# The second product of the MLP: for six of eight output tiles, twelve of 22 chunks by 2x2 blocks with seven products each

## The chip, the cores and the metric

One core of a Trainium2 chip. The metric is the device time of one execution in microseconds (us); the kernel before took 664.03 us, the median of three runs (663.77 to 664.38).

## The reference, cut to what matters

One transformer block on 512 tokens, D = 1024, in float32: attention, then a gated MLP with a causal convolution, then a gated per-layer input. The change is in the product with `w_down`, whose inner size is D_FF = 2816 = 22 chunks of 128:

```python
gu = h @ w_gate_up[i]
a, u = jnp.split(gu, [D_FF], axis=-1)
a = causal_dwconv(a, conv_w[i], conv_b[i])
y = (jax.nn.gelu(a, approximate=True) * u) @ w_down[i]     # (512 x 2816) @ (2816 x 1024)
x = x + rmsnorm(y, mlp_post_g[i])
e = p[i] @ w_ple[i]
x = x + e * jax.nn.sigmoid(x @ w_ple_gate[i])
```

## The kernel before

Everything is held transposed: features on the 128 partitions, the 512 tokens along the free axis. Every fp32 product is made of three fp32r matmuls, since each operand is split into a high and a low half: `mm3` (L138 to L149) issues hi·hi (L145), lo·hi (L148) and hi·lo (L149), each with a 128x128 weight and 512 (or 256) columns of tokens.

`weight()` brings a weight in: SP issues the load into one of two `wr` buffers (L138), ACT copies the high half out (L126), DVE subtracts it to get the low half (L130). The halves live in six `wh` slots, so three weights of up to 1024 columns; the split of a weight waits until PE is done with the weight three before it, and the next load waits until a split has freed its `wr`.

`mlp_up` makes the 22 chunks of the MLP's inner vector. `mlp_tile(j)` (L1006 to L1022) leaves chunk j as a pair of halves in `self.y[j]`; the first four chunks come from one joint product, the rest one by one. `mlp_down` multiplies them with `w_down`: for each of eight output tiles `c`, three weights of 1024, 1024 and 768 columns (8, 8 and 6 chunks) are loaded, split and multiplied into one PSUM bank with 22 x 3 matmuls of 512 columns. DVE copies the bank out (L1092), ACT squares it (L266) and POOL adds the square to a running sum (L267) for the RMS norm. The last tile, c = 7, is done in two halves of 256 tokens, so that the norm of the first half runs under the second half's matmuls (`last`, `out`). Three of the gate's weights (`wpg`, loaded at c = 2, 3 and 4, and split into free slots of other buffers) and a fourth wait for the product of the gate that follows; `norm_half` adds the normed result to x (`self.x1`, four tiles of 128x2x512), and `gated` adds e (`self.e`, p @ w_ple, four such tiles).

The instruction order on each engine comes from the framework's scheduler, which orders by priority and its own timing; instructions given to `keep_in_program_order` (`keep`, `load_late`) stay in the order of the code. Within a queue nothing overtakes.

## Time and profile before

| | |
|---|---|
| median of 3 runs | 664.03 us (663.77 to 664.38) |
| the profiled execution | 663.63 us, of which the span is 661.8 us |
| granted TensorE clock | 0.999 of full speed |
| PE, share of the span | 99% |
| DVE / ACT / POOL | 61% / 49% / 25% |
| second product of the MLP | 490.0 to 611.9 us of the span |
| DMA | 69.56 MB, mean 105 GB/s |

Matmuls are pipelined, so the duration in a matmul's row (0.39 us at 512 columns) is not what it adds: that is the distance from one start to the next. All times in rows are us from the start of the span, unless marked ns.

### The profile page before, as it was taken

The page shows a single profiled execution, that of the slowest core. Times are in us where ns is not written, and L with a number is a line of the kernel's source. Part 1 is how long each engine was busy: PE and PEld are TensorE (multiplying, and loading weights), DVE is VectorE, ACT ScalarE, POOL GpSimd, SP SyncE. Part 2 cuts the span into 40 slices and gives each one's busy share as a digit, 9 for nine tenths or more (in the row PEclk, how much of TensorE's full clock was granted, in tenths as well). Part 3 has the DMA queues.
Part 4 walks back from the last instruction along what each step waited for, and adds up shares of the span by engine and source line. Part 5 has one row for each costly group of instructions (what it writes and reads, how often), then busy time and mean ns, then how long its engine had stood idle before and what let it go on. Part 6 is the DMA issues. An engine that isn't in the chain of part 4 may idle for free.

```text
span 661.8 us, 9234 instructions
## 1 busy us (share of the span) xinstructions
PE 654.4 (99%) x3287; PEld 551.4 (83%) x3287; DVE 404.4 (61%) x832; ACT 326.7 (49%) x606; POOL 166.7 (25%) x248
## 2 busy tenths in 40 slices
...
GB/s 302 172 108 205 185 65 55 58 21 70 58 240 139 128 130 29 65 64 96 108 95 105 98 103 97 97 95 97 95 88 88 123 140 119 88 102 82 2 111 81
DMA packets 25070, 69.56 MB, mean 105 GB/s; under 512 B 3136, under 2 KB 5184, under 8 KB 25024
## 3 DMA queue, kind: packets, MB, share of 16 engines
...
q14 instruction: 20, 0.16, 0.1%
q10 hardware_dynamic: 144, 0.08, 0.1%
...
## 4 chain that ended last, share of the span: by engine, by line
PE 92%; DVE 4%; ACT 2%; POOL 1%; issue 1%; DMA 1%; SPq 0%; ACTq 0%; DVEq 0%
PE mlpup_pss L148 4%; PE mlpup_pss L145 4%; PE mlpup_pss L149 4%; PE mlpup_psmm L148 3%; PE mlpup_pst L148 3%; PE mlpup_psmm L145 3%; PE mlpup_pst L145 3%; PE mlpup_pst L149 3%; PE mlpup_psmm L149 3%; PE mlpdown_pss L149 3%; PE mlpdown_pss L145 3%; PE mlpdown_pss L148 3%; PE mlpdown_psmm L145 2%; PE mlpdown_psmm L149 2%; PE mlpdown_psmm L148 2%; PE nsa_pso L589 2%
## 5 line engine op out<-in xcount | busy, mean ns | idle before, releaser
L1017 POOL TENSOR_TENSOR mlpup_s<-mlpup_s,r3b 128x512 f32<-128x512 f32 x22 | 29.7, 1349 | 214.8 <-ACT mlpup_s L1016 214.8
L126 ACT ACTIVATE mlpup_wh<-mlpup_wr 128x1024 fp32r<-128x1024 f32 x38 | 40.3, 1061 | 75.0 <-PE mlpup_pss L148 37.6
L126 ACT ACTIVATE mlpdown_wh<-mlpdown_wr 128x1024 fp32r<-128x1024 f32 (+1 forms) x28 | 28.0, 1000 | 84.7 <-PE mlpdown_pss L148 30.1
L130 DVE TENSOR_TENSOR mlpdown_wh<-mlpdown_wr,mlpdown_wh 128x1024 fp32r<-128x1024 f32 (+1 forms) x28 | 32.9, 1176 | 60.0 <-ACT mlpdown_wh L126 60.0
L130 DVE TENSOR_TENSOR mlpup_wh<-mlpup_wr,mlpup_wh 128x1024 fp32r<-128x1024 f32 x38 | 47.3, 1244 | 4.7 <-ACT mlpup_wh L126 4.6
L145 PE MATMUL mlpup_pss<-r_u,mlpup_wh 128*128 128x512 f32 x120 | 46.7, 389 | 0.0
L148 PE MATMUL mlpup_pss<-r_u,mlpup_wh 128*128 128x512 f32 x120 | 46.7, 389 | 0.0
L149 PE MATMUL mlpup_pss<-r_u,mlpup_wh 128*128 128x512 f32 x120 | 46.7, 389 | 0.0
L579 POOL TENSOR_SCALAR nsa_u<-nsa_u,nsa_nrc,gate 128x512 f32<-128x512 f32 (+3 forms) x64 | 38.5, 618 | 14.8 <-DVE nsa_nrc L715 9.7
L681 ACT ACTIVATE nsa_u<-nsa_u,nsa_nnm 128x512 f32<-128x512 f32 (+3 forms) x64 | 35.4, 555 | 6.8 <-DVE nsa_nnm L674 6.6
L561 DVE TENSOR_TENSOR nsa_u<-nsa_pst,nsa_u 128x512 fp32r<-128x512 f32 (+1 forms) x43 | 29.4, 685 | 6.8 <-ACT nsa_u L558 6.5
L267 POOL TENSOR_TENSOR mlpdown_s<-mlpdown_s,mlpdown_s 128x512 f32<-128x512 f32 x6 | 7.8, 1297 | 100.3 <-ACT mlpdown_s L266 100.3
L149 PE MATMUL mlpdown_pss<-mlpup_u,mlpdown_wh 128*128 128x512 f32 (+1 forms) x88 | 32.0, 364 | 0.0
L145 PE MATMUL mlpdown_pss<-mlpup_u,mlpdown_wh 128*128 128x512 f32 (+1 forms) x88 | 32.0, 364 | 0.0
L148 PE MATMUL mlpdown_pss<-mlpup_u,mlpdown_wh 128*128 128x512 f32 (+1 forms) x88 | 31.9, 363 | 0.0
L1016 ACT ACTIVATE mlpup_s<-mlpup_s 128x512 f32<-128x512 f32 x22 | 13.9, 631 | 35.5 <-DVE mlpup_s L1015 35.5
L130 POOL TENSOR_TENSOR fill_wh<-fill_wr,fill_wh 128x1024 fp32r<-128x1024 f32 (+2 forms) x13 | 24.6, 1894 | 26.5 <-ACT fill_wh L126 26.5
L145 PE MATMUL mlpup_pst<-r_u,mlpup_wh 128*128 128x512 f32 x80 | 31.1, 389 | 0.0
L148 PE MATMUL mlpup_pst<-r_u,mlpup_wh 128*128 128x512 f32 x80 | 31.1, 389 | 0.0
L149 PE MATMUL mlpup_pst<-r_u,mlpup_wh 128*128 128x512 f32 x80 | 31.1, 389 | 0.0
L145 PE MATMUL mlpup_psmm<-r_u,mlpup_wh 128*128 128x512 f32 x80 | 31.1, 389 | 0.0
L148 PE MATMUL mlpup_psmm<-r_u,mlpup_wh 128*128 128x512 f32 x80 | 31.1, 389 | 0.0
...
## 6 DMA issues: line engine op xcount, KB each, us to landing
mlpup_wr<-in_gu_dram SPq DMA_DIRECT2D x38, 512.0 KB, 3.3
mlpdown_wr<-in_down_dram SPq DMA_DIRECT2D x16, 512.0 KB, 3.6
fill_wr<-in_win_dram SPq DMA_DIRECT2D x6, 512.0 KB, 3.6
...
fill_u<-fill_u SPq DMA_DIRECT2D x20, 128.0 KB, 2.7
...
compress_u<-projk_u SPq DMA_DIRECT2D x16, 128.0 KB, 2.3
mlpdown_wr<-in_wpg_dram SPq DMA_DIRECT2D x4, 512.0 KB, 3.3
```

What stands on the lines that cost most here:

```text
L126: h = nc.scalar.activation(hi, raw, AF.Copy)
L130: l = eng.tensor_sub(lw, raw, hi.bitcast(F32))
L145: r = self.pin(mm(ps, hi, x[:, 0, :], start=start, stop=False))
L148: mm(ps, lo, x[:, 0, :], start=False, stop=False)
L149: mm(ps, hi, x[:, 1, :], start=False, stop=stop)
L267: (eng or (nc.vector if last else nc.gpsimd)).tensor_add(acc, acc, sq)
L561: nc.vector.tensor_sub(t[rs, part, :], pt[rs], t[rs, 0, :].bitcast(F32))
L579: self.nc.gpsimd.tensor_scalar(ap, ap, col, gate, op0=ALU.mult, op1=ALU.mult)
L589: self.att(nc.tensor.matmul(po, v, t[:, part, :], start=start, stop=stop))
L681: nc.scalar.activation(dst, dst, AF.Exp, bias=nm[:, r, b : b + 1], scale=-1.0, accum_out=sm[:, r, b : b + 1])
L1016: nc.scalar.activation(c0, c0, AF.Gelu_apprx_tanh)
L1017: nc.gpsimd.tensor_mul(c0, c0, self.r3)
```

## The change

Six output tiles are taken as three pairs, (0,1), (2,3), (4,5). For a pair, chunks 0 to 11 are taken as six pairs too, and the 512 tokens as two halves of 256. That gives 2x2 blocks on every side, and each of the 18 block products is made by the Winograd form of Strassen's scheme: seven products of a 128x128 weight with 256 tokens (`block_products`) where the plain way has eight. The operands and the results need sums:

- on the weights (`block_weight`): a 256 KB load brings the four blocks, four dependent DVE subtractions and additions of 128 columns make three more (L1068 to L1071 of the changed kernel), and the 896 columns are split by ACT and DVE as before;
- on the chunks (`sums`): for each pair of chunks four DVE operations of 256 columns, one ACT copy of 256, two ACT copies and two DVE subtractions of 512. For chunks 0 to 7 they stand in `mlp_tile`; for 8 to 11 they are made early in the second product (`sums_late`), after four more additions of 512 on DVE, which put the chunk together from its halves;
- on the results (`block_sums`): six PSUM banks are summed to the two tiles by one ACT copy and four DVE additions of 256 columns and two of 512.

Chunks 12 to 21 stay plain 512-column matmuls, with one weight for both tiles (1024, 768, 768 columns). `ORDER` says how plain parts and blocks alternate. Loads go round five buffers (`rawtag`). Tile 6 is as before, with two of the gate's weights loaded between its own; tile 7 is as before, with the third one after its first weight.

The sums of chunks 0 to 7 need room: x and e are written to DRAM in `mlp_up` (`spill`, eight transfers of 512 KB) and read back, x after the blocks of the third pair, e after the loads of tile 7 (`unspill`).

```diff
@@ -61 +63 @@
+KP = 6
+EARLY = 4
+MP = 3
+ORDER = [[range(0, 4), (), range(4, 6)], [range(0, 3), range(3, 6), ()], [range(6), (), ()]]
+TTAG = ["pt", "u", "u", "u", "p", "p", "p", "p"]
@@ -1006 +1015 @@
+    def spill(self):
+        self.kept = {}
+        for key, ts in (("e", self.e), ("x1", self.x1)):
+            self.kept[key] = []
+            for i, t in enumerate(ts):
+                d = self.dp.tile([P, 2, T], F32, name=f"kept_{key}{i}")
+                self.load_late(d, t)
+                self.kept[key].append(d)
+        self.e = self.x1 = None
+    def unspill(self, key, tags):
+        r = []
+        for d, tag in zip(self.kept[key], tags):
+            t = self.u([P, 2, T], F32, tag)
+            self.load_late(t, d)
+            r.append(t)
+        return r
+    def sums(self, j, c):
+        nc = self.nc
+        a, b = slice(0, H), slice(H, T)
+        if j % 2 == 0:
+            tags = TTAG[j : j + 2] if j < 2 * EARLY else ["u", "u"]
+            self.tt.append([self.u([P, 2, T], F32R, t) for t in tags])
+            self.sum = self.u([P, 2, T], F32, "kn" if j == 2 * EARLY else "u")
+        ta, tb = self.tt[j // 2]
+        ra, rb = (self.sum[:, i, :] for i in range(2))
+        if j % 2 == 0:
+            nc.vector.tensor_sub(ra[:, a], c[:, b], c[:, a])
+            nc.scalar.activation(rb[:, a], c[:, b], AF.Copy)
+        else:
+            nc.vector.tensor_sub(ra[:, b], c[:, b], ra[:, a])
+            nc.vector.tensor_sub(rb[:, a], c[:, b], rb[:, a])
+            nc.vector.tensor_sub(rb[:, b], c[:, a], ra[:, b])
+            for t, r in ((ta, ra), (tb, rb)):
+                nc.scalar.activation(t[:, 0, :], r, AF.Copy)
+                nc.vector.tensor_sub(t[:, 1, :], r, t[:, 0, :].bitcast(F32))
+    def sums_late(self):
+        for j in range(2 * EARLY, 2 * KP):
+            c = self.s([P, T])
+            self.nc.vector.tensor_add(c, self.y[j][:, 0, :].bitcast(F32), self.y[j][:, 1, :].bitcast(F32))
+            self.sums(j, c)
+    def block_weight(self, c, i, tag):
+        nc = self.nc
+        r = self.wrp.tile([P, 7 * P], F32, tag="wr", name=self.nm("wr")) if tag == "wr" else self.u([P, 7 * P], F32, tag)
+        src = self.io["down"][c : c + 2, :, 2 * i * P : (2 * i + 2) * P].rearrange("c p n -> p c n")
+        nc.sync.dma_start(r[:, : 4 * P].rearrange("p (c n) -> p c n", c=2), src)
+        b = [r[:, k * P : (k + 1) * P] for k in range(7)]
+        nc.vector.tensor_sub(b[4], b[0], b[2])
+        nc.vector.tensor_add(b[2], b[2], b[3])
+        nc.vector.tensor_sub(b[5], b[2], b[0])
+        nc.vector.tensor_sub(b[6], b[1], b[5])
+        return self.weight(r, 7 * P, early=True)
+    def block_products(self, c, i, wt, banks, last=False):
+        d, e, p1, p5, p6, p7 = banks
+        y1, y2 = self.y[2 * i], self.y[2 * i + 1]
+        ta, tb = self.tt[i]
+        a, b = slice(0, H), slice(H, T)
+        for ps, k, x in ((p1, 0, y1[:, :, a]), (p6, 5, ta[:, :, b]), (p7, 4, tb[:, :, a]), (p5, 2, ta[:, :, a])):
+            self.mm3(ps[:, a], wt, k * P, x, i == 0, i == KP - 1)
+        for ps, k, x in ((d[:, a], 1, y2[:, :, a]), (d[:, b], 6, y2[:, :, b]), (e[:, a], 3, tb[:, :, b])):
+            self.mm3(ps, wt, k * P, x, False, last and k != 1)
+    def block_sums(self, m, banks):
+        nc = self.nc
+        d, e, p1, p5, p6, p7 = banks
+        a, b = slice(0, H), slice(H, T)
+        t = self.s([P, H])
+        nc.scalar.activation(m[:, 0, a], p1[:, a], AF.Copy)
+        nc.vector.tensor_add(t, m[:, 0, a], p6[:, a])
+        nc.vector.tensor_add(m[:, 1, a], t, p7[:, a])
+        nc.vector.tensor_add(m[:, 0, b], t, p5[:, a])
+        nc.vector.tensor_add(m[:, 1, b], m[:, 1, a], p5[:, a])
+    def pair_of_tiles(self, c, m, acc):
+        nc, io = self.nc, self.io
+        t = ("t", "mm", "t")[c // 2]
+        banks = [self.ps(k) for k in (t, t, "s", "s", "s", "o")]
+        gs = [range(12, 16), range(16, 19), range(19, NFF)]
+        def plain(js):
+            src = io["down"][c : c + 2, :, js.start * P : js.stop * P].rearrange("c p n -> p c n")
+            w = self.weight(self.raw(src, 2 * len(js) * P, next(self.rawtag)), 2 * len(js) * P, early=True)
+            for k, ps in enumerate(banks[:2]):
+                for n, j in enumerate(js):
+                    self.mm3(ps, w, (k * len(js) + n) * P, self.y[j], j == 2 * KP, j == NFF - 1 and not more)
+        def blocks(ks):
+            for i in ks:
+                self.block_products(c, i, self.block_weight(c, i, next(self.rawtag)), banks, more and i == KP - 1)
+        more = len(ORDER[c // 2][2]) > 0
+        for js, ks in zip(gs, ORDER[c // 2]):
+            plain(js)
+            blocks(ks)
+            if c == 0 and js is gs[0]:
+                self.sums_late()
+            if c == 2 * MP - 2 and len(ks):
+                self.tt = None
+                self.x1 = self.unspill("x1", ["p"] * 4)
+        self.block_sums(m, banks)
+        for k in range(2):
+            nc.vector.tensor_add(m[:, k, :], m[:, k, :], banks[k])
+            self.square_acc(acc, m[:, k, :], c + k == 0)
@@ -1022 +1144 @@
+        if j < 2 * EARLY:
+            self.sums(j, c0)
@@ -1049 +1173 @@
+        self.tt = []
@@ -1057 +1182 @@
+        self.spill()
@@ -1082 +1207 @@
-        for c in range(KC):
+        self.rawtag = itertools.cycle(["wr", "wr", "u", "kn", "tt"])
+        for c in range(0, 2 * MP, 2):
+            self.pair_of_tiles(c, yo[c // 2], acc)
+        for c in range(2 * MP, KC - 1):
@@ -1084 +1212 @@
-            wts = []
-            if c < KC - 1:
-                ps = self.ps(self.ROT[c % 8])
-                for k in ks:
-                    wt = self.weight(io["down"][c][:, k.start * P : k.stop * P], len(k) * P)
-                    self.gemm(ps, wt, [self.y[j] for j in k], k.start == 0, k.stop == NFF)
-                if 2 <= c < 5:
-                    self.pgw.append(self.weight(io["wpg"][c - 2], tag=("u", "u", ("kn", "tt"))[c - 2]))
-                nc.vector.tensor_copy(m, ps)
-                self.square_acc(acc, m, c == 0)
+            ps = self.ps("mm")
+            for n, k in enumerate(ks):
+                wt = self.weight(io["down"][c][:, k.start * P : k.stop * P], len(k) * P)
+                self.gemm(ps, wt, [self.y[j] for j in k], k.start == 0, k.stop == NFF)
+                if n < 2:
+                    self.pgw.append(self.weight(io["wpg"][n], tag="u"))
+            nc.vector.tensor_copy(m, ps)
+            self.square_acc(acc, m, c == 0)
@@ -1097 +1223 @@
-        wts = [self.weight(io["down"][c][:, k.start * P : k.stop * P], len(k) * P) for k in ks]
+        wts = []
+        for n, k in enumerate(ks):
+            wts.append(self.weight(io["down"][c][:, k.start * P : k.stop * P], len(k) * P))
+            if n == 0:
+                self.pgw.append(self.weight(io["wpg"][2], tag=("kn", "tt")))
@@ -1098 +1229 @@
+        self.e = self.unspill("e", ["pt", "u", "u", "u"])
```

Where instructions move, at three places (names: `mlpdown_wh` a weight's half, `mlpup_u` a chunk's halves or sums, `pss`, `pso`, `pst`, `psmm` PSUM banks). First PE, early in the second product. Before, six matmuls of tile 0 (its chunks 7 and 8):

```order
L145 MATMUL mlpdown_psmm_899_4766<-mlpup_u_753_3736,mlpdown_wh_901_4769 128x512
L148 MATMUL mlpdown_psmm_899_4766<-mlpup_u_753_3736,mlpdown_wh_902_4770 128x512
L149 MATMUL mlpdown_psmm_899_4766<-mlpup_u_753_3736,mlpdown_wh_901_4769 128x512
L145 MATMUL mlpdown_psmm_899_4766<-mlpup_u_763_3809,mlpdown_wh_904_4799 128x512
L148 MATMUL mlpdown_psmm_899_4766<-mlpup_u_763_3809,mlpdown_wh_905_4800 128x512
L149 MATMUL mlpdown_psmm_899_4766<-mlpup_u_763_3809,mlpdown_wh_904_4799 128x512
```

Now, the end of the first plain part (two tiles, four chunks each) and the first two products of block 0:

```order
L153 MATMUL mlpdown_pst_912_4833<-mlpup_u_845_4386,mlpdown_wh_918_4840 128x512
L156 MATMUL mlpdown_pst_912_4833<-mlpup_u_845_4386,mlpdown_wh_919_4841 128x512
L157 MATMUL mlpdown_pst_912_4833<-mlpup_u_845_4386,mlpdown_wh_918_4840 128x512
L153 MATMUL mlpdown_pss_913_4834<-mlpup_u_704_3354,mlpdown_wh_921_4874 128x256
L156 MATMUL mlpdown_pss_913_4834<-mlpup_u_704_3354,mlpdown_wh_922_4875 128x256
L157 MATMUL mlpdown_pss_913_4834<-mlpup_u_704_3354,mlpdown_wh_921_4874 128x256
L153 MATMUL mlpdown_pss_915_4836<-mlpup_u_705_3357,mlpdown_wh_921_4874 128x256
L156 MATMUL mlpdown_pss_915_4836<-mlpup_u_705_3357,mlpdown_wh_922_4875 128x256
L157 MATMUL mlpdown_pss_915_4836<-mlpup_u_705_3357,mlpdown_wh_921_4874 128x256
```

Up to the first matmul of the second product PE's order is the same in both; from there to the start of tile 6 each block's 21 matmuls of 128x256 stand for 12 of 128x512, and the products of a block go to different banks. In all PE has 162 instructions more (378 of 256 columns in, 216 of 512 out).

Second DVE, in the first 35 us of the second product. Before, from the fourth weight's low half on:

```order
L130 TENSOR_TENSOR mlpdown_wh_912_4857<-mlpdown_wr_910_4854,mlpdown_wh_911_4856 128x1024
L130 TENSOR_TENSOR mlpdown_wh_915_4887<-mlpdown_wr_913_4884,mlpdown_wh_914_4886 128x1024
L1092 COPY mlpdown_u_895_4762<-mlpdown_psmm_899_4766 128x512
L130 TENSOR_TENSOR mlpdown_wh_918_4917<-mlpdown_wr_916_4914,mlpdown_wh_917_4916 128x768
L130 TENSOR_TENSOR mlpdown_wh_923_4946<-mlpdown_wr_921_4943,mlpdown_wh_922_4945 128x1024
L130 TENSOR_TENSOR mlpdown_wh_926_4976<-mlpdown_wr_924_4973,mlpdown_wh_925_4975 128x1024
```

Now, from the low half of block 1's weight to that of block 3's; the whole piece has three rows of 896 columns, eight of 128, four of 512 and six of 256, shown in two parts that join:

```order
L138 TENSOR_TENSOR mlpdown_wh_925_4906<-mlpdown_u_923_4899,mlpdown_wh_924_4905 128x896
L1068 TENSOR_TENSOR mlpdown_u_926_4930<-mlpdown_u_926_4930 128x128
L1069 TENSOR_TENSOR mlpdown_u_926_4930<-mlpdown_u_926_4930 128x128
L1070 TENSOR_TENSOR mlpdown_u_926_4930<-mlpdown_u_926_4930 128x128
L1139 TENSOR_TENSOR mlpup_s_904_4817<-mlpup_psmm_903_4791,mlpup_s_904_4817 128x512
L1071 TENSOR_TENSOR mlpdown_u_926_4930<-mlpdown_u_926_4930 128x128
L1142 TENSOR_TENSOR mlpup_u_905_4824<-mlpup_s_904_4817,mlpup_u_905_4824 128x512
L1058 TENSOR_TENSOR mlpdown_s_941_5015<-mlpup_u_805_4094 128x512
L1068 TENSOR_TENSOR mlpdown_u_929_4961<-mlpdown_u_929_4961 128x128
L138 TENSOR_TENSOR mlpdown_wh_928_4937<-mlpdown_u_926_4930,mlpdown_wh_927_4936 128x896
L1069 TENSOR_TENSOR mlpdown_u_929_4961<-mlpdown_u_929_4961 128x128
L1045 TENSOR_TENSOR mlpdown_u_935_4996<-mlpdown_s_932_4992 128x256
```

and on from there:

```order
L1070 TENSOR_TENSOR mlpdown_u_929_4961<-mlpdown_u_929_4961 128x128
L1049 TENSOR_TENSOR mlpdown_u_935_4996<-mlpdown_s_936_4999,mlpdown_u_935_4996 128x256
L1048 TENSOR_TENSOR mlpdown_u_935_4996<-mlpdown_s_936_4999,mlpdown_u_935_4996 128x256
L1071 TENSOR_TENSOR mlpdown_u_929_4961<-mlpdown_u_929_4961 128x128
L1050 TENSOR_TENSOR mlpdown_u_935_4996<-mlpdown_s_936_4999,mlpdown_u_935_4996 128x256
L1045 TENSOR_TENSOR mlpdown_u_940_5012<-mlpdown_s_937_5008 128x256
L1053 TENSOR_TENSOR mlpdown_u_933_4994<-mlpdown_u_935_4996,mlpdown_u_933_4994 128x512
L1048 TENSOR_TENSOR mlpdown_u_940_5012<-mlpdown_s_941_5015,mlpdown_u_940_5012 128x256
L138 TENSOR_TENSOR mlpdown_wh_931_4968<-mlpdown_u_929_4961,mlpdown_wh_930_4967 128x896
```

Before, a weight's low half followed a weight's low half. Now the sums of the next blocks' weights (L1068 to L1071), what is left of the last chunk (L1139, L1142) and the sums of chunks 8 to 11 (L1058, L1045 to L1053) stand between the low halves, and a low half waits for all that is ahead of it.

Third SP's queue, the loads from the last weights of tile 5 on. Before, from the third gate weight:

```order
L138 DMA mlpdown_wr_958_5217<-in_wpg_dram 128x1024
L138 DMA mlpdown_wr_963_5228<-in_down_dram 128x1024
L138 DMA mlpdown_wr_966_5258<-in_down_dram 128x1024
L138 DMA mlpdown_wr_969_5288<-in_down_dram 128x768
L138 DMA mlpdown_wr_974_5317<-in_down_dram 128x1024
L138 DMA mlpdown_wr_977_5347<-in_down_dram 128x1024
L138 DMA mlpdown_wr_980_5377<-in_down_dram 128x768
L138 DMA mlpdown_wr_984_5405<-in_down_dram 128x1024
```

Now, from the last two weights of the third pair:

```order
L146 DMA mlpdown_wr_1023_5660<-in_down_dram 128x2x384
L146 DMA mlpdown_wr_1026_5684<-in_down_dram 128x2x384
L279 DMA mlpdown_u_1019_5652<-kept_x10_3296 128x1024
L279 DMA mlpdown_u_1020_5654<-kept_x11_3298 128x1024
L279 DMA mlpdown_u_1021_5656<-kept_x12_3300 128x1024
L279 DMA mlpdown_u_1022_5658<-kept_x13_3302 128x1024
L146 DMA mlpdown_wr_1033_5723<-in_down_dram 128x1024
L146 DMA mlpdown_wr_1036_5753<-in_wpg_dram 128x1024
L146 DMA mlpdown_wr_1039_5759<-in_down_dram 128x1024
L146 DMA mlpdown_wr_1042_5789<-in_wpg_dram 128x1024
L146 DMA mlpdown_wr_1045_5795<-in_down_dram 128x768
```

Four reads of x (`kept_x1`) stand ahead of tile 6's first weight, and the gate's weights now stand between those of tiles 6 and 7 where before they had gone earlier.

## Rows read from the trace of the kernel before

**Rows 1.** The page: the span, the busy time of each engine with its share of the span and its instructions (part 1), and the chain that ended last, by engine (part 4).

```profile
span 661.8 us, 9234 instructions
...
PE 654.4 (99%) x3287; PEld 551.4 (83%) x3287; DVE 404.4 (61%) x832; ACT 326.7 (49%) x606; POOL 166.7 (25%) x248
...
PE 92%; DVE 4%; ACT 2%; POOL 1%; issue 1%; DMA 1%; SPq 0%; ACTq 0%; DVEq 0%
```

**Rows 2.** The timeline of PE, single matmuls: start in us from the span's start, duration, line, output and operands, output shape. The last of the first product (mlpup), the first of the second product and the one 36 matmuls later, the first of tile 1, the first of the last tile's two halves of 256 tokens, which are 66 matmuls apart, and two matmuls of the gate that are 7 apart.

```profile
489.75 0.39 PE L149 MATMUL mlpup_psmm<-r_u,mlpup_wh 128*128 128x512 f32 x1
489.97 0.39 PE L145 MATMUL mlpdown_psmm<-mlpup_u,mlpdown_wh 128*128 128x512 f32 x1
...
498.13 0.39 PE L145 MATMUL mlpdown_psmm<-mlpup_u,mlpdown_wh 128*128 128x512 f32 x1
...
505.04 0.39 PE L145 MATMUL mlpdown_pss<-mlpup_u,mlpdown_wh 128*128 128x512 f32 x1
...
595.44 0.28 PE L145 MATMUL mlpdown_pss<-mlpup_u,mlpdown_wh 128*128 128x256 f32 x1
...
603.33 0.28 PE L145 MATMUL mlpdown_psmm<-mlpup_u,mlpdown_wh 128*128 128x256 f32 x1
...
621.09 0.28 PE L1037 MATMUL norm_pss<-norm_u,mlpdown_wh 128*128 128x256 f32 x1
...
621.92 0.28 PE L1038 MATMUL norm_psmm<-norm_u,mlpdown_wh 128*128 128x256 f32 x1
```

**Rows 3.** The windows view, one row for each stretch of the span: busy us and instructions of PE, PEld, DVE, ACT and POOL, granted clock of PE, DMA share, GB/s. The second product runs from 490 to 612.

```profile
260.00:300.00 40.00, 40.00 (x178) 33.10 (x177) 31.81 (x37) 17.90 (x23) 3.25 (x3) 1.00 0.16 53
300.00:400.00 100.00, 100.00 (x443) 82.78 (x442) 60.69 (x74) 40.84 (x51) 14.79 (x11) 1.00 0.30 100
...
500.00:540.00 40.00, 40.00 (x177) 32.87 (x176) 13.86 (x13) 11.76 (x13) 2.62 (x2) 1.00 0.38 114
540.00:560.00 20.00, 20.00 (x90) 16.45 (x89) 6.81 (x6) 5.63 (x6) 1.30 (x1) 1.00 0.47 133
...
600.00:620.00 20.00, 20.00 (x171) 20.00 (x170) 11.53 (x30) 4.64 (x10) 1.41 (x2) 1.00 0.09 29
```

**Rows 4.** Groups of DVE instructions by line and form from 240 us to the end: output and operands, shapes, count, busy us, mean ns of one, idle us before them and releaser.

```profile
L130 DVE TENSOR_TENSOR mlpdown_wh<-mlpdown_wr,mlpdown_wh 128x1024 fp32r<-128x1024 f32 x20 | 25.3, 1263 | 60.0 <-ACT mlpdown_wh L126 60.0
...
L1018 DVE TENSOR_TENSOR mlpup_s<-mlpup_psmm,mlpup_s 128x512 f32<-128x512 f32 x12 | 8.3, 690 | 21.2 <-POOL mlpup_s L1017 21.2
L130 DVE TENSOR_TENSOR mlpdown_wh<-mlpdown_wr,mlpdown_wh 128x768 fp32r<-128x768 f32 x8 | 7.7, 957 | 0.0
...
L979 DVE TENSOR_TENSOR swa_u<-swa_u,mlpdown_u 128x256 f32<-128x256 f32 x8 | 3.4, 425 | 0.3
```

**Rows 5.** The same of ACT.

```profile
L126 ACT ACTIVATE mlpdown_wh<-mlpdown_wr 128x1024 fp32r<-128x1024 f32 x20 | 21.2, 1061 | 62.4 <-PE mlpdown_pss L148 20.9 <-PE mlpdown_psmm L148 18.1 <-PE mlpdown_pst L148 15.6
...
L1020 ACT ACTIVATE mlpup_u<-mlpup_s 128x512 fp32r<-128x512 f32 x22 | 13.9, 634 | 10.8 <-DVE mlpup_s L1018 9.8
...
L126 ACT ACTIVATE mlpdown_wh<-mlpdown_wr 128x768 fp32r<-128x768 f32 x8 | 6.8, 847 | 22.3 <-PE mlpdown_pss L148 9.1 <-PE mlpdown_psmm L148 6.1 <-PE mlpdown_pst L148 6.1
...
L980 ACT ACTIVATE norm_u<-outproj_u 128x256 fp32r<-128x256 f32 x8 | 3.3, 418 | 8.0 <-DVE outproj_u L979 8.0
```

**Rows 6.** Waits from 480 us to the end: engine, line waited in, releaser; us in total, times, the longest.

```profile
DVE mlpdown_wh L130 <- ACT mlpdown_wh L126: 60.0, 19, 4.7
ACT mlpdown_wh L126 <- PE mlpdown_pss L148: 30.1, 8, 4.4
```

**Rows 7.** The same for the queue of DMA issues on SP.

```profile
SPq L138 <- DVE mlpdown_wh L130: 118.2, 28, 11.4
...
SPq L138 <- DMA mlpdown_wr<-in_down_dram: 3.6, 4, 1.0
```

**Rows 8.** The timeline of DVE: a weight's low half, then two instructions on another buffer, the second of which uses what the first wrote.

```profile
485.65 1.23 DVE L130 TENSOR_TENSOR mlpdown_wh<-mlpdown_wr,mlpdown_wh 128x1024 fp32r<-128x1024 f32 x1 [0.22 <-ACT mlpdown_wh L126]
486.79 0.75 DVE L1014 SCALAR_TENSOR_TENSOR mlpup_s<-mlpup_u,cols,mlpup_s 128x512 f32<-128x512 f32 x1
487.57 0.75 DVE L1015 SCALAR_TENSOR_TENSOR mlpup_s<-mlpup_u,cols,mlpup_s 128x512 f32<-128x512 f32 x1
```

**Rows 9.** The timeline of SP from 240 us to 272 us: the loads issued there, from the first one's issue to the last one's.

```profile
244.98 24.80 SPq L138 DMA_DIRECT2D mlpup_wr<-in_gu_dram  x3
```

**Rows 10.** The DMA view of 240 us to 300 us: GB/s in 40 equal slices of 1.5 us.

```profile
GB/s 0 0 0 16 314 216 153 11 0 0 0 0 0 0 0 0 0 0 0 0 235 120 238 112 0 11 0 0 0 0 0 298 52 5 49 300 0 0 0 0
```

**Rows 11.** The source view of L944, where DVE adds the attention's output to x: durations in ns, start of the first and of the last, forms.

```profile
L944 DVE TENSOR_TENSOR outproj_u<-outproj_u,swa_u x4: 691/691/692, 255.7 to 262.9; 128x512 f32<-128x512 f32 x4
```

**Rows 12.** The windows view, as rows 3, of stretches with several transfers in flight.

```profile
3.00:6.00 3.00, 2.88 (x9) 1.84 (x7) 1.26 (x4) 0.82 (x2) 1.23 (x8) 1.00 1.03 310
...
12.00:15.00 3.00, 3.00 (x18) 3.00 (x17) 3.00 (x6) 2.88 (x6) 0.00 (x0) 1.00 1.05 413
...
190.00:195.00 5.00, 5.00 (x27) 4.23 (x26) 1.62 (x6) 3.10 (x7) 4.04 (x7) 1.00 0.90 313
219.00:222.00 3.00, 3.00 (x15) 2.49 (x14) 2.26 (x4) 2.50 (x5) 0.74 (x1) 1.00 0.90 275
```

**Rows 13.** DMA issues (part 6 of the page): transfer, queue, count, KB each, median us from issue to landing.

```profile
mlpdown_wr<-in_down_dram SPq DMA_DIRECT2D x16, 512.0 KB, 3.6
...
fill_u<-fill_u SPq DMA_DIRECT2D x20, 128.0 KB, 2.7
...
mlpdown_wr<-in_wpg_dram SPq DMA_DIRECT2D x4, 512.0 KB, 3.3
```

2 lines of the change are left out of this document (added).

## The prediction

> **What bounds the kernel now.** I read the page first, then the timeline of PE, then the windows, then the groups, waits and transfers of the two engines that feed PE. [...] PE's own price is the distance between starts [rows 2]: 36 matmuls of 512 columns take 498.13 - 489.97 = 8.16 us, so 0.2267 each; 66 matmuls of 256 columns take 603.33 - 595.44 = 7.89 us, so 0.1195 each. That is more than half of 0.2267 (0.1133): a matmul of half the columns costs 53% of a whole one. PEld shows why to be careful with more, smaller matmuls: 20.00 of 20 us busy in 600 to 620, where the halves run, against 32.87 of 40 in 500 to 540 [rows 3].
>
> **The change, part by part.**
>
> *Matmuls.* The order shows 216 matmuls of 512 columns out and 378 of 256 in. Out: 216 x 0.2267 = 48.97 us. In: 378 x 0.1195 = 45.17 us. Sum **-3.80 us**; per block 21 x 0.1195 = 2.51 against 12 x 0.2267 = 2.72. All of it lies on the path, since PE never waits in this stretch. The saving of 1/8 in products shrinks to 8% because the halves cost 53%. Two matmuls of the gate, which alternate between banks as a block's products do, give (621.92 - 621.09)/7 = 0.1186 [rows 2]; with that the sum is 48.97 - 44.83 = -4.14, the lower end. I take 0.1195, since it was measured on the same product and chunks.
>
> *Sums on the chunks, 0 to 7.* For each pair DVE 4 x 0.425 + 2 x 0.69 = 3.08 us [rows 4] and ACT 0.42 + 2 x 0.634 = 1.69 [rows 5]; four pairs 12.3 and 6.7 us. They run beside the first product: DVE has 8.2 us idle in 260 to 300 and 39.3 in 300 to 400 [rows 3], ACT more. The first two pairs (6.2 us) fall in the busier stretch. Cost 0. If the cover were gone, a weight's low half would be late by what is missing.
>
> *Block weights.* Each: four DVE operations of 128 columns, whose duration no row shows. From 690 at 512 and 425 at 256 [rows 4] the line goes to 425 - 132 = 0.29 us; the ends are 0.16 (where that line meets no columns) and 0.425 (a row of twice the size). I take 0.29. The split of 896 columns lies between the rows of 768 and 1024: DVE 1.09 (0.957 to 1.263), ACT 0.95 (0.847 to 1.061) [rows 4, 5]. So DVE has 4 x 0.29 + 1.09 = 2.25 us per block where PE has 2.51, but the plain parts give it 13.6 us per pair in which it splits for 3.15. Before, each split found room: DVE waited 60.0 us in 19 times for ACT's half, and ACT waited for PE by up to 4.4 us a time [rows 6]. Cost 0, with the rival below for the first pair, which also carries the sums of chunks 8 to 11 (4 x 0.69 + 2 x 3.08 = 8.9 us).
>
> *Sums on the results.* One ACT copy and four DVE operations, 0.42 + 1.70 = 2.1 us, free the banks of the seven products. The next pair starts with a plain part in other banks, 24 x 0.2267 = 5.44 us, which covers it. Cost 0; without that cover 2.1 us per pair.
>
> *x and e to DRAM and back.* Eight writes of 512 KB stand in SP's queue behind a load and ahead of one that before was issued at 269.45 at the end of a run that began at 244.98 (244.98 + 24.80, less the 0.33 of an issue) [rows 9]; the DMA engines move nothing from 252 to 270 [rows 10]. 4.19 MB at the 275 to 413 GB/s of stretches with several transfers in flight [rows 12] take 10 to 15 us. The last part of x is written by 263.6 [rows 11], which leaves the last write 5.8 us against the 3.3 to 3.6 that 512 KB take to land [rows 13]. Cost 0. The reads come back while the last tiles run; that is the second rival.
>
> *More and smaller loads.* 18 loads of 256 KB, one per 2.51 us, are 104 GB/s, the rate of the stage before (114 to 133 GB/s in 500 to 560 [rows 3]), and stand up to five deep in the queue. Loads of 128 KB land after 2.7 us, of 512 KB after 3.6 [rows 13]. The queue waited 118.2 us for buffers to come free and 3.6 us for data [rows 7]: it was not the limit. Cost 0.
>
> **Sum.** 663.63 (profiled execution, span 661.8) - 3.80 = 659.83. The median of the runs shown is 0.40 above that execution, so the forecast is **660.2 us**.
>
> **The rivals.**
>
> *A. DVE is late in the first pair.* The low half of block 1's weight cannot start before the last weight of the first product is done: 489.97, plus ACT's 0.95, gives 490.95 [rows 2, 5]. From there to the end of block 3's low half the order puts 3 x 1.09 + 8 x 0.29 + 4 x 0.69 + 6 x 0.425 = 10.9 us on DVE. PE comes to that half at 489.97 + 5.44 + 3 x 2.51 + 0.12 = 503.06. That leaves 1.2 us. Over the whole first pair, to the first block of the second, I count 24.9 us of DVE work in 27.7 us. With 0.425 in place of 0.29, and 0.03 us more for an operation that uses what the one before wrote (start to start 0.78 for a duration of 0.75 [rows 8]), 24 operations cost 4.0 us more: 28.9 in 27.7, so 1.2 us late. Then 661.4 us; twice that is 662.6. Against it: the line through two rows is good to a few per cent, and DVE starts an independent instruction before the last one's end (486.79, where 485.65 + 1.23 is 486.88 [rows 8]). [...] Chance 0.16.
>
> *B. The late reads crowd the last weights: slower.* A pair takes 60 x 0.2267 + 126 x 0.1195 = 28.66 us. x's buffers come free with the third pair's third and fourth block, from 489.97 + 2 x 28.66 + 5.44 + 3 x 2.51 = 560.3 on; tile 7's third weight is needed 48 halves into that tile, at 489.97 + 3 x 28.66 + 15.07 (tile 6, as tile 0 before: 505.04 - 489.97 [rows 2]) + 48 x 0.1195 = 596.8, and must have landed some 4 us earlier. Between the two SP's queue has 12.5 transfers of 512 KB: four of x, 2.75 of tile 6, three of the gate, 2.75 of tile 7. That is 6.55 MB in 32.5 us, 202 GB/s, where the stage had 114 to 133 [rows 3]. Each may take 2.60 us. From there PE waits; at 32.5 + 3.8 = 36.3 us, 2.90 us each, the gain is gone; if they go one after the other at 3.3 us each [rows 13], they take 41.25 us, 8.75 late: **669 us**. For it: the reads stand ahead of tile 6's first weight in the queue, nothing overtakes, and two buffers hold the loads behind. Against it: with several in flight the same queue moved 275 to 413 GB/s [rows 12], and the reads of x need no split, so all four can be in flight. Chance 0.12, more than half of it slower than before.
>
> *C. Halves at half the price.* If what makes a half dear in tile 7 (0.1195 against 0.1133) were missing in a block, where the products alternate between banks, 378 x 0.1133 = 42.83 would come in and 6.14 go: 657.9 us. The gate's halves, which alternate too, speak against it (0.1186). Chance 0.03. [...]
>
> That the change would not do what it says is out: the order shows the matmuls gone and added, and PE's order ahead of the second product the same.
>
> **How the numbers follow.** A measurement of this kernel can tell about 0.2% (1.33 us) from no change: faster is below 662.70, slower above 665.36. Forecast 0.66, all faster. A: 0.13 faster, 0.03 within. B: 0.01 faster, 0.04 within, 0.07 slower. C: 0.03, faster. What I have not named: 0.03, a third each. Faster 0.84, same 0.08, slower 0.08. The range goes from 659.2 (0.1186 for a half, -4.14, gives 659.9; less 0.3 for the spread of the runs and as much again for a rate between the gate's and half the price) to 663.0 (A twice, 662.6, and the spread); it leaves out C and most of B, about 0.15.
>
> **What would show it.** Right: in the changed kernel's timeline 21 matmuls of a block lie 2.51 us apart in all, PE is busy throughout from 490 to the norm, tile 7's halves start about 3.8 us earlier (595.44 to 591.6), and the second product is the only part that is shorter. A would show as PE idle ahead of a block in 500 to 518 with DVE's low half as releaser, DVE at over 90% there, and 128-column rows above 0.4 us. B would show as PE idle in tile 6 or 7 behind an ACT or DVE half that waited for a transfer. Wrong would be a rate of the halves in blocks above 0.125 (no gain from 0.1295 on, 48.97/378), or lost time in the first product from 270 to 300.

## The result, and the profile of the changed kernel

| | before | changed |
|---|---|---|
| median | 664.09 us (6 runs, 663.67 to 664.38) | 659.85 us (6 runs, 659.56 to 660.81) |
| ratio | | 0.9939, 95% interval 0.9926 to 0.9952 |
| profiled execution | 663.63, span 661.8 | 659.60, span 657.9 |
| second product of the MLP | 489.97 to 611.87, 121.90 us | 490.05 to 608.05, 118.00 us |

Forecast was 660.2 (659.2 to 663.0), faster. Two repeats beside the experiments gave ratios of 0.9942 (0.9930 to 0.9955) and 0.9930 (0.9917 to 0.9942).

The changed kernel's page: span, busy times, chain by engine.

```profile
span 657.9 us, 9783 instructions
...
PE 650.7 (99%) x3449; PEld 556.3 (85%) x3449; DVE 452.6 (69%) x965; ACT 342.1 (52%) x636; POOL 171.6 (26%) x248
...
PE 93%; DVE 4%; ACT 2%; POOL 1%; issue 1%; ACTq 0%; DVEq 0%
```

Against [rows 1] PE is busy 3.7 us less and the span is 3.9 us shorter; DVE has gone from 404.4 to 452.6 us and ACT from 326.7 to 342.1 without showing in the span. That is the whole result in three lines: only PE's time counted.

PE's timeline, the first matmul of each stretch: the first plain part, the six blocks of the third pair, the plain parts behind them, tile 7, the gate.

```profile
490.05 0.39 PE L153 MATMUL mlpdown_pst<-mlpup_u,mlpdown_wh 128*128 128x512 f32 x1
...
553.26 0.28 PE L153 MATMUL mlpdown_pss<-mlpup_u,mlpdown_wh 128*128 128x256 f32 x1
...
568.28 0.40 PE L153 MATMUL mlpdown_pst<-mlpup_u,mlpdown_wh 128*128 128x512 f32 x1
...
591.62 0.28 PE L153 MATMUL mlpdown_pss<-mlpup_u,mlpdown_wh 128*128 128x256 f32 x1
...
608.05 0.28 PE L1160 MATMUL norm_pss<-norm_u,mlpdown_wh 128*128 128x256 f32 x1
```

They answer to [rows 2]. The third pair's six blocks take 568.28 - 553.26 = 15.02 us, 126 matmuls, 0.1192 each; all 18 blocks 45.10 us, against 45.17 in the forecast. The 216 matmuls that went had taken 48.96 us in the trace of before (48.97 in the forecast), and the plain parts of the three pairs take 41.41 us where the same matmuls had taken 41.44. Tile 7 starts 3.82 us earlier (595.44 before). The second product is 3.90 us shorter; the rest of the span is the same within 0.1.

The windows:

```profile
260.00:300.00 40.00, 40.00 (x178) 33.12 (x177) 31.79 (x37) 17.97 (x24) 2.86 (x3) 1.00 0.22 73
300.00:400.00 100.00, 100.00 (x443) 82.84 (x442) 70.30 (x98) 45.58 (x62) 17.57 (x11) 1.00 0.31 100
490.00:500.00 10.00, 10.00 (x62) 8.94 (x62) 7.86 (x18) 4.00 (x6) 1.68 (x1) 1.00 0.17 53
500.00:510.00 10.00, 10.00 (x69) 9.18 (x68) 8.00 (x18) 4.41 (x8) 0.00 (x0) 1.00 0.54 160
510.00:520.00 10.00, 10.00 (x65) 9.14 (x64) 7.46 (x18) 5.04 (x6) 0.00 (x0) 1.00 0.40 110
520.00:550.00 30.00, 30.00 (x192) 27.25 (x191) 22.30 (x54) 11.10 (x14) 1.96 (x2) 1.00 0.31 95
550.00:580.00 30.00, 30.00 (x193) 27.26 (x192) 16.44 (x21) 10.44 (x12) 4.26 (x3) 1.00 0.52 167
580.00:600.00 20.00, 20.00 (x123) 17.91 (x122) 7.50 (x7) 6.35 (x9) 3.56 (x3) 1.00 0.69 222
```

PE is busy throughout at a granted clock of 1.00, as in [rows 3]. DVE, at 13.86 of 40 us there before, is now at 7.86, 8.00 and 7.46 of 10 in the first pair. In 260 to 300 it is no busier than before (31.79 against 31.81): the sums on the first chunks fell behind 300 (70.30 against 60.69).

Two waits from 480 us on:

```profile
DVE mlpdown_wh L138 <- ACT mlpdown_wh L134: 29.2, 20, 2.8
...
ACT mlpdown_wh L134 <- DMA mlpdown_wr<-in_down_dram: 14.7, 6, 3.9
```

DVE's waiting for ACT fell from 60.0 to 29.2 us [rows 6]; ACT now waits 14.7 us for loads, where before it had waited 3.0 in all. The cover has become thinner on both sides, but no matmul waits. The closest places, found by setting each low half's end against the first matmul that reads it, have 1.3 to 1.6 us left: block 3 of the first pair is one. Its low half ends at 502.26 on DVE:

```profile
491.07 1.09 DVE L138 TENSOR_TENSOR mlpdown_wh<-mlpdown_u,mlpdown_wh 128x896 fp32r<-128x896 f32 x1 [1.31 <-ACT mlpdown_wh L134]
492.63 0.83 DVE L1068 TENSOR_TENSOR mlpdown_u<-mlpdown_u 128x128 f32<-128x128 f32 x1 [0.47 <-DMA mlpdown_u<-in_down_dram]
...
496.75 0.28 DVE L1068 TENSOR_TENSOR mlpdown_u<-mlpdown_u 128x128 f32<-128x128 f32 x1
496.95 1.08 DVE L138 TENSOR_TENSOR mlpdown_wh<-mlpdown_u,mlpdown_wh 128x896 fp32r<-128x896 f32 x1
...
501.18 1.08 DVE L138 TENSOR_TENSOR mlpdown_wh<-mlpdown_u,mlpdown_wh 128x896 fp32r<-128x896 f32 x1
```

and PE reads it first at 503.80 (the first of these rows is the start of the block):

```profile
503.09 0.40 PE L153 MATMUL mlpdown_pss<-mlpup_u,mlpdown_wh 128*128 128x256 f32 x2
...
503.80 0.29 PE L156 MATMUL mlpdown_pss<-mlpup_u,mlpdown_wh 128*128 128x256 f32 x1
```

Another is tile 7's second weight, 1.34 us where before it had 4.80.

The last writes of x in SP's queue; the next load is issued at 269.51, as before (269.45, the end of the run of [rows 9]):

```profile
258.48 5.55 SPq L279 DMA_DIRECT2D kept_x<-outproj_u  x2
269.51 0.33 SPq L146 DMA_DIRECT2D mlpup_wr<-in_gu_dram  x1
```

### The profile page after: what moved, and what is told of

It is laid out like the page before. It is cut to its first block, busy times and chain, and to the rows that moved or that the text cites. A ratio compares the mean times of both kernels' runs of the same rounds, so it can differ in the third digit from the quotient of the medians.

```text
span 657.9 us, 9783 instructions
## 1 busy us (share of the span) xinstructions
PE 650.7 (99%) x3449; PEld 556.3 (85%) x3449; DVE 452.6 (69%) x965; ACT 342.1 (52%) x636; POOL 171.6 (26%) x248
## 4 chain that ended last, share of the span: by engine, by line
PE 93%; DVE 4%; ACT 2%; POOL 1%; issue 1%; ACTq 0%; DVEq 0%
PE mlpup_pss L156 4%; PE mlpup_pss L153 4%; PE mlpup_pss L157 4%; PE mlpup_psmm L156 3%; PE mlpup_pst L156 3%; PE mlpup_psmm L153 3%; PE mlpup_pst L153 3%; PE mlpup_pst L157 3%; PE mlpup_psmm L157 3%; PE mlpdown_psmm L153 2%; PE mlpdown_psmm L157 2%; PE mlpdown_psmm L156 2%; PE mlpdown_pst L157 2%; PE mlpdown_pst L153 2%; PE mlpdown_pst L156 2%; PE nsa_pso L597 2%
## 5 line engine op out<-in xcount | busy, mean ns | idle before, releaser
L1138 POOL TENSOR_TENSOR mlpup_s<-mlpup_s,r3b 128x512 f32<-128x512 f32 x22 | 32.5, 1475 | 215.0 <-ACT mlpup_s L1137 215.0
L587 POOL TENSOR_SCALAR nsa_u<-nsa_u,nsa_nrc,gate 128x512 f32<-128x512 f32 (+3 forms) x64 | 38.6, 615 | 14.7 <-DVE nsa_nrc L723 9.6
L134 ACT ACTIVATE mlpdown_wh<-mlpdown_wr 128x1024 fp32r<-128x1024 f32 (+2 forms) x22 | 21.3, 968 | 40.6 <-DMA mlpdown_wr<-in_down_dram 14.7
L138 DVE TENSOR_TENSOR mlpdown_wh<-mlpdown_wr,mlpdown_wh 128x1024 fp32r<-128x1024 f32 (+2 forms) x22 | 24.4, 1111 | 20.7 <-ACT mlpdown_wh L134 20.7
L275 POOL TENSOR_TENSOR mlpdown_s<-mlpdown_s,mlpdown_s 128x512 f32<-128x512 f32 x6 | 9.8, 1630 | 93.0 <-ACT mlpdown_s L274 92.9
L153 PE MATMUL mlpup_psmm<-r_u,mlpup_wh 128*128 128x512 f32 x80 | 31.1, 389 | 0.0
L156 PE MATMUL mlpup_psmm<-r_u,mlpup_wh 128*128 128x512 f32 x80 | 31.1, 389 | 0.0
L157 PE MATMUL mlpup_psmm<-r_u,mlpup_wh 128*128 128x512 f32 x80 | 31.1, 389 | 0.0
L682 DVE CUSTOM_DVE_ANT_0 nsa_u<-nsa_pss,biastables_u 128x224 f32<-128x224 f32 (+3 forms) x64 | 27.8, 446 | 3.0 <-PE nsa_pss L623 2.4
L566 ACT ACTIVATE nsa_u<-nsa_pst 128x512 fp32r<-128x512 f32 x43 | 25.4, 593 | 8.5 <-PE nsa_pst L564 7.9
```

The costliest lines, as they stand in the source:

```text
L134: h = nc.scalar.activation(hi, raw, AF.Copy)
L138: l = eng.tensor_sub(lw, raw, hi.bitcast(F32))
L153: r = self.pin(mm(ps, hi, x[:, 0, :], start=start, stop=False))
L156: mm(ps, lo, x[:, 0, :], start=False, stop=False)
L157: mm(ps, hi, x[:, 1, :], start=False, stop=stop)
L566: nc.scalar.activation(t[:, 0, :], pt, AF.Copy)
```

## The experiments

Theory 1: PE's products alone set the time, and all that was added is hidden, though not by much. Against it stand that the added work costs something which cheaper halves make up for (e1), and that DVE (e3, e6, e7) or the queue (e4) is already the limit or far from it. e5 asks why a half is dear; e6 and e8 try for more of the gain. Margins and waits below are read from the profile of each run; the changed kernel's second product takes 118.00 us in its own profile and 118.01 in both repeats.

**e1 and e1b: the products put back, everything else kept.** The edit, in `block_products` (e1 with `ta, tb` for `y1, y2`), with `block_sums` fed from the plain bank:

```diff
-        for ps, k, x in ((p1, 0, y1[:, :, a]), (p6, 5, ta[:, :, b]), ...
+        for ps, k, x in ((d, 0, y1), (d, 1, y2), (e, 2, y1), (e, 3, y2)):
+            self.mm3(ps, wt, k * P, x, False, last and k % 2 == 1)
```

> The changed kernel with a block's seven products put back to four whole ones: 12 matmuls of 512 columns in place of 21 of 256 (on the first four columns blocks of the weight and on the sums of the chunks, so the output is not the reference's). All else stays: the sums on chunks and weights, 896-column splits, loads, reads and writes of x and e, sums on results. Theory 1 (only PE's matmuls count, all that was added is hidden): + 18 x 12 x 0.2267 - 45.10 = +3.87, so 663.7 us, as the kernel before (664.1) within 0.5. Rival 2 (the added work costs something, and the halves are cheaper than they look): above 664.6, and the excess over the kernel before is that cost. Rival 3 (the gain came from the moved loads or another order): it stays near 660.

Measured: 665.40 us, ratio to the kernel before 1.0022 (1.0013 to 1.0031), above what theory 1 gave and within what rival 2 gave. In its profile the second product took 123.81 us, 5.81 more than in the changed kernel. Tile 7 takes 1.41 us of this, behind one wait of 0.88 for the low half of its second weight; the 216 matmuls take 49.55 us, 4.45 more than the changed kernel's blocks, so 0.2294 each, not 0.2267; the plain parts take 0.05 less. (The expectation of e1b below puts 1.0 on tile 7 and the rest on the matmuls, hence its 0.2309 and its 0.9.) e1 read the sums' buffers. That left two readings, so e1b reads the chunks.

> As e1, but the 12 whole matmuls of a block read the chunks themselves, not the sums (the sums are still made, and read by nothing; the weight's third block is the sum, so the output is not the reference's). e1 came out 5.8 us above the changed kernel in its profile, of which 1.0 was one wait in tile 7; its 216 whole matmuls took 0.2309 each where the same matmuls on the chunks took 0.2267 in the kernel before. Theory 1: read from the chunks they cost 0.2267 again, so +3.87 over the changed kernel, within 0.3, and no more than the kernel before. Rival (the added work on DVE, ACT and in the queue slows PE's stream, whatever the operands): 0.2309 each, +4.8, 0.9 above the kernel before.

Measured: 663.81 us, ratio to the kernel before 0.9998 (0.9989 to 1.0007); second product 121.83 us, so 3.83 more than the changed kernel's 118.00, no wait on PE. Its first matmul and the first of the norm behind it:

```profile
490.28 0.39 PE L153 MATMUL mlpdown_pst<-mlpup_u,mlpdown_wh 128*128 128x512 f32 x1
...
612.11 0.28 PE L1159 MATMUL norm_pss<-norm_u,mlpdown_wh 128*128 128x256 f32 x1
```

The 216 matmuls take 49.03 us, 0.2270 each. All the added work on DVE and ACT, all the loads, the writes and reads of x and e are in this kernel, and it takes what the kernel before took. One thing stands elsewhere: no matmul reads the sums here, so their buffers come free sooner, and the reads of x are issued from 548.91 on, 11 us earlier than in the changed kernel (559.91). That the reads cost nothing at their own place is therefore not shown by e1b; it is shown by the changed kernel's own trace, in which no matmul waits. With that, what was added costs nothing, and the gain is PE's products alone. Of e1's excess, 0.52 us goes with the operands it read; its 1.41 us in tile 7, where the reads of x stand as late as in the changed kernel, was not taken apart.

**e3: more work on DVE.** Edit in `block_weight`:

```diff
         nc.vector.tensor_sub(b[6], b[1], b[5])
+        for k in range(4):
+            nc.vector.tensor_sub(b[6], b[1], b[5])
```

> The changed kernel with the last of the four 128-column operations on a block's weight done five times: four more DVE operations per block, 0.20 to 0.29 us each, so 0.8 to 1.15 us per block, 14 to 21 us in all. Theory 1 (DVE has a margin of about 1.5 us at the first pair's blocks 3 and 4, more elsewhere): two blocks' worth, 1.6 to 2.3 us, stands ahead of block 3's low half, so PE waits 0.1 to 0.8 there and about as much again at one or two later places: 660.2 to 662. Rival (DVE is far from being late): 659.9. Rival (DVE already sets the pace): + 14 or more, 674.

Measured: 666.80 us, ratio to before 1.0052 (1.0035 to 1.0070): slower, and by more than I expected. PE's timeline, the places where it waits:

```profile
505.96 0.39 PE L156 MATMUL mlpdown_pss<-mlpup_u,mlpdown_wh 128*128 128x256 f32 x1 [0.96 <-DVE mlpdown_wh L138]
...
517.86 0.39 PE L153 MATMUL mlpdown_pss<-mlpup_u,mlpdown_wh 128*128 128x256 f32 x1 [1.61 <-ACT mlpdown_wh L134]
```

It waits for block 3's low half (0.96), for the first half of a weight at block 4 (1.61, ACT behind DVE's sums) and at a few places more, 3.9 us together; the second product takes 124.13 us, 6.13 more. Most of the rest is clock: after the wait at 516 the granted clock is 0.66 over 518 to 522 and 0.96 over 522 to 530, as an estimate 4 x 0.34 = 1.4 and 8 x 0.04 = 0.3 us. Four operations a block are more than the margin, as theory 1 had it at block 3, but I had not counted that the wait at block 4 grows with each weight ahead of it, nor the clock.

**e4: x read back twice.** Edit in `pair_of_tiles`, behind `unspill`:

```diff
+                for t, k in zip(self.x1, self.kept["x1"]):
+                    self.load_late(t, k)
```

> The changed kernel with x read back twice, the second time right behind the first in SP's queue: 2.1 MB more ahead of tile 6's first weight. In the changed kernel the low halves of tiles 6 and 7 end 1.3 to 3.6 us ahead of their use. Rival B's theory (the reads crowd the last weights): 2.1 MB at 275 to 413 GB/s are 5 to 7.6 us more ahead of tile 6's weights, less the 3 us of slack: 2 to 4.5 us late, 662 to 664.5. Theory 1 in its strong form (the queue has room for it): 659.9.

Measured: 665.82 us (663.23 to 666.48 over ten runs), ratio to before 1.0024 (1.0014 to 1.0035): rival B's mechanism, at the upper end of its price and beyond. PE's timeline in tile 7, at its second weight:

```profile
596.21 0.38 PE L153 MATMUL mlpdown_pss<-mlpup_u,mlpdown_wh 128*128 128x256 f32 x1 [1.22 <-ACT mlpdown_wh L134]
597.76 0.58 PE L156 MATMUL mlpdown_pss<-mlpup_u,mlpdown_wh 128*128 128x256 f32 x1 [1.16 <-DVE mlpdown_wh L138]
```

and the windows there:

```profile
596.00:598.00 2.00, 0.63 (x2) 0.43 (x3) 1.51 (x1) 0.88 (x2) 0.62 (x1) 0.90 0.22 89
598.00:600.00 2.00, 2.00 (x10) 2.00 (x11) 0.96 (x1) 0.12 (x1) 0.00 (x0) 0.50 0.59 170
600.00:602.00 2.00, 2.00 (x15) 2.00 (x14) 0.00 (x0) 0.00 (x0) 0.00 (x0) 0.75 0.92 371
```

PE waits 1.22 us for the high half and 1.16 for the low one. The load of this weight was issued at 590.79, 3.3 us later than in the changed kernel (587.45), while tile 7 began only 0.3 later: that part is the queue. ACT's timeline shows a second reason:

```profile
594.58 0.63 ACT L274 ACTIVATE mlpdown_s<-mlpdown_u 128x512 f32<-128x512 f32 x1 [1.90 <-DVE mlpdown_u L1220]
595.12 1.04 ACT L134 ACTIVATE mlpdown_wh<-mlpdown_wr 128x1024 fp32r<-128x1024 f32 x1
```

The square of tile 6 (L274) stands ahead of the high half here, and behind it in the changed kernel. There ACT took the weight 3.51 us after its load was issued (587.45 to 590.96, waiting for it); as an estimate from that, it could have started at 594.3 here, so some 0.8 us of the waits are ACT's order and not the queue. Then the matmuls of 256 columns follow at 0.21 in place of 0.12: the granted clock is 0.50 over 598 to 600, 0.75 in the next 2 us and 1.00 again after that. Of the 4.33 us that the second product lost in this profile, 2.8 are waits and the rest is the clock behind them (0.50 for 2 us and 0.75 for 2 more are 1.5 us). The profiled execution took 664.16 us, 1.7 less than the median of the ten, so the trace shows less than the median lost.

**e5: why a half costs 53%.** Edit: two matmuls of 128 columns for each of 256.

```diff
-            self.mm3(ps[:, a], wt, k * P, x, i == 0, i == KP - 1)
+            for q in (slice(0, P), slice(P, 2 * P)):
+                self.mm3(ps[:, q], wt, k * P, x[:, :, q], i == 0 and q.start == 0, i == KP - 1 and q.start > 0)
```

> The changed kernel with each of a block's products made by two matmuls of 128 columns in place of one of 256: 756 in place of 378. What makes a half cost 53%? If each matmul has a fixed cost beside its columns (a line through 0.2267 at 512 and 0.1193 at 256: 0.0119 + 0.419 ns per column), one of 128 costs 0.0656 and the sum is 49.6 against 45.1: +4.5, 664.3. If the weight load bounds the halves (loads start every 0.12 us there and PEld is busy throughout), each still costs 0.12: 90.7, +45.6, 705. Between the two: a load takes less than 0.12 but more than 0.066.

Measured: 698.92 us, ratio to before 1.0529 (1.0513 to 1.0544). The second product takes 157.34 us; the 756 matmuls of 128 columns take 84.16 us of it, 0.1113 each, where the 378 of 256 took 45.10:

```profile
500.99 0.28 PE L153 MATMUL mlpdown_pss<-mlpup_u,mlpdown_wh 128*128 128x128 f32 x1
501.11 0.28 PE L156 MATMUL mlpdown_pss<-mlpup_u,mlpdown_wh 128*128 128x128 f32 x1
```

So a quarter of the columns costs almost what a half costs (0.1193), and the weight loads stand at the same distance (0.11 us from start to start, 500.82 to 500.93) with PEld busy throughout (5.00 of 5 us):

```profile
500.00:505.00 5.00, 5.00 (x47) 5.00 (x47) 4.80 (x10) 2.96 (x6) 0.00 (x0) 1.00 0.42 112
```

Of the two readings the load's is the nearer: a matmul with a load of its own costs 0.1113 at 128 columns, and a half lies 7% above that. No run tried fewer columns, and what makes up the 7% is not shown.

**e6: seven pairs of chunks.** Edit: `KP = 7`, plain chunks 14 to 21, four buffers for loads in place of five, output tiles allotted when needed, and

```diff
-            self.nc.vector.tensor_add(c, self.y[j][:, 0, :].bitcast(F32), self.y[j][:, 1, :].bitcast(F32))
+            self.nc.gpsimd.tensor_add(c, self.y[j][:, 0, :].bitcast(F32), self.y[j][:, 1, :].bitcast(F32))
```

> The changed kernel with seven pairs of chunks by blocks in place of six (21 blocks, plain chunks 14 to 21 in two weights of 1024 columns), the additions that put chunks 8 to 13 together on POOL in place of DVE, output tiles allotted when they are needed, and four buffers for loads in place of five. Theory 1: a block is worth 2.72 - 2.505 = 0.21 us as long as DVE keeps up: three more blocks, -0.65, so 0.6 us below the changed kernel on this chip. Rival A again (DVE late in the first pair, which has six sums of chunks and seven weights now, some 27 of 28.4 us): PE waits 1 to 3 us there, and it is 0.4 to 2.5 above the changed kernel, more where the clock falls.

Measured: 664.55 us, ratio to before 1.0008 (0.9999 to 1.0017): rival A come true, the gain gone. The windows in the first pair, PE's busy time the first column, the granted clock behind POOL's:

```profile
502.00:504.00 2.00, 0.97 (x6) 0.77 (x6) 2.00 (x4) 1.18 (x3) 0.26 (x1) 1.00 0.00 0
504.00:506.00 2.00, 0.53 (x3) 0.53 (x4) 2.00 (x5) 2.00 (x4) 0.00 (x0) 0.91 0.48 127
506.00:508.00 2.00, 2.00 (x11) 2.00 (x11) 2.00 (x4) 0.42 (x1) 0.00 (x0) 0.50 0.52 139
```

PE stands still for about half of 502 to 504 and most of 504 to 506, then runs at clock 0.50. The second product takes 122.18 us. DVE is busy throughout, and some of its rows are too long; its timeline, then POOL's:

```profile
498.16 0.41 DVE L1049 TENSOR_TENSOR mlpdown_u<-mlpdown_s,mlpdown_u 128x256 f32<-128x256 f32 x1
498.50 1.51 DVE L1048 TENSOR_TENSOR mlpdown_u<-mlpdown_s,mlpdown_u 128x256 f32<-128x256 f32 x1
...
501.01 1.80 DVE L1053 TENSOR_TENSOR mlpdown_u<-mlpdown_u,mlpdown_u 128x512 fp32r<-128x512 f32 x1
...
503.06 0.68 DVE L1053 TENSOR_TENSOR mlpdown_u<-mlpdown_u,mlpdown_u 128x512 fp32r<-128x512 f32 x1
```

```profile
498.18 1.54 POOL L1058 TENSOR_TENSOR mlpdown_s<-mlpup_u 128x512 f32<-128x512 f32 x1 [1.63 <-DVE mlpdown_u L1045]
500.69 1.56 POOL L1058 TENSOR_TENSOR mlpdown_s<-mlpup_u 128x512 f32<-128x512 f32 x1 [0.97 <-DVE mlpdown_u L1050]
```

An operation of 256 columns takes 0.41 us at 498.16 and 1.51 at 498.50, one of 512 takes 1.80 at 501.01 and 0.68 at 503.06: each long one stands beside one of POOL's additions. Moving an operation to POOL did not take it off DVE. The next two runs take the two apart in part: e7 has the additions on POOL without the seventh pair, e8 the seventh pair without POOL, but not in the first pair of tiles.

**e7: only the four additions on POOL**, the edit above in the changed kernel.

> The changed kernel with one edit: the four additions that put chunks 8 to 11 together run on POOL in place of DVE. In e6 every such POOL addition (1.3 to 1.56 us) stood beside a DVE operation that took about 1.1 us longer than others of its form (1.51 for 0.41, 1.80 for 0.68, 2.02 for 1.08). Theory (while POOL runs, DVE stands still for most of it): DVE saves 4 x 0.61 = 2.4 us and loses about 4 x 1.1 = 4.4, so it is up to 2 us later in the first pair, where its margin was 1.5 us: 659.9 to 661, with four DVE rows about 1.1 us too long beside the POOL rows. Rival (e6 was only too much DVE work, POOL is free): DVE is 2.4 us earlier, the time stays at 659.9, and no such rows.

Measured: 660.69 us (four runs, 659.89 to 661.43), ratio to before 0.9948 (0.9932 to 0.9963), beside 659.76 for the changed kernel on that chip. DVE's timeline, then POOL's:

```profile
479.88 1.27 DVE L1069 TENSOR_TENSOR mlpdown_wr<-mlpdown_wr 128x128 f32<-128x128 f32 x1
481.19 1.29 DVE L1070 TENSOR_TENSOR mlpdown_wr<-mlpdown_wr 128x128 f32<-128x128 f32 x1
...
485.76 1.70 DVE L138 TENSOR_TENSOR mlpdown_wh<-mlpdown_wr,mlpdown_wh 128x896 fp32r<-128x896 f32 x1
...
496.41 1.27 DVE L1069 TENSOR_TENSOR mlpdown_u<-mlpdown_u 128x128 f32<-128x128 f32 x1
```

```profile
479.66 2.67 POOL L1058 TENSOR_TENSOR mlpdown_s<-mlpup_u 128x512 f32<-128x512 f32 x2
485.22 1.29 POOL L1058 TENSOR_TENSOR mlpdown_s<-mlpup_u 128x512 f32<-128x512 f32 x1 [2.89 <-DVE mlpup_u L1142]
...
496.05 1.48 POOL L1058 TENSOR_TENSOR mlpdown_s<-mlpup_u 128x512 f32<-128x512 f32 x1 [5.11 <-DVE mlpup_u L1142]
```

All four additions stand beside a DVE row that is too long: operations of 128 columns take 1.27 to 1.29 us (0.28 elsewhere), and a low half of 896 columns takes 1.70 (1.09 elsewhere). These are the four rows that the theory asked for and the rival did not have, by 0.6 to 1.0 us each and not 1.1. Three of them stand ahead of the second product, where DVE had room. The smallest margin in the second product fell from 1.34 us (tile 7's second weight) to 0.57 (the third block of the second pair, 1.46 before), and the second product took 118.15. The direction is the theory's; the time alone could not tell it from the rival.

**e8: seven pairs where DVE has room.** Six in the first pair of tiles, seven in the second and third, additions on DVE.

```diff
+KPS = [6, 7, 7]
-                self.sums_late()
+                self.sums_late(range(2 * EARLY, 2 * KPS[0]))
+            if c == 2 and js is gs[0]:
+                self.sums_late(range(2 * KPS[0], 2 * KPS[1]))
```

> Seven pairs of chunks by blocks in the second and third pair of tiles only, six in the first; the sums of chunks 12 and 13 are made in the second pair; the additions stay on DVE. Two more blocks than the changed kernel, 2 x 0.21 = 0.43 us less on PE. Theory 1 (e6 failed for DVE in the first pair alone): 0.4 us below the changed kernel, PE never waits, the second product takes 117.57 in place of 118.00 us. Rival (a seventh block is too much for DVE in the second pair as well): PE waits there about 530, by 0.5 to 3 us, and it is slower than the changed kernel.

Measured: 659.73 us (659.22 to 660.09) against 659.76 (659.57 to 659.94) for the changed kernel on the same chip. In the profile the second product took 117.42 us, 0.58 less than 118.00 (0.43 expected), with no wait on PE. The whole does not show it: in that profile the second product began at 490.44, in the changed kernel's repeat at 489.98. So theory 1 holds for the stage, and as a version it is no faster by what these runs can tell.

## Why the prediction was right

- **Matmuls, -3.80.** The step held: the second product is 3.90 us shorter, the blocks cost 0.1193 a matmul (0.1195 taken), and e1b, with the products alone put back, returns to 0.9998 of the kernel before. Rival C did not come true.
- **Costs at nothing.** e1b carries every added operation and transfer, the reads of x 11 us earlier, and costs nothing over the kernel before; in the changed kernel itself no matmul waits. They were not taken out one by one; e3 and e4 show for DVE's sums and for the reads that the cover ends not far off.
- **Block weights.** 0.285 us for 128 columns (0.29 taken), 1.09 for 896. On DVE the next independent operation starts after 0.20 (496.75 to 496.95), so the pace was better than I took: over the first pair I had counted 24.9 us of DVE work in 27.7, and the windows from 490 to 520 show 23.3 busy of 30.
- **Rival A, 1.2 us of margin.** It was 1.54, for reasons I had not counted: I let PE need the low half with the block's second matmul. The order puts six of the block's hi·hi matmuls ahead of it (503.09 to 503.80), which I could have seen. One of DVE's operations took 0.83 in place of 0.28, beside POOL's row of 1.68; that took part of it back. The mechanism is real: e3 and e6 set it off.
- **Rival B.** The queue kept up at 167 GB/s in 550 to 580 and 222 in 580 to 600. I had looked at tile 7's third weight; the close one was the second (1.34 us). The mechanism is real: 2.1 MB more, and e4 was slower than the kernel before. I had left the clock out of its price. Part of e4's wait is ACT's order and not the queue.
- **Sum.** The profiled execution moved by 4.03, the medians by 4.24 us, within the interval of the ratio (3.2 to 4.9). Two small slips in the sums change nothing: 489.97 + 0.95 is 490.92, and the low end of the range adds up to 659.3.

What stays open: why a whole matmul costs 0.2267 in some places and 0.228 to 0.235 in others (0.5 us of e1). In the kernel before it goes by the chunk, within a nanosecond in each tile: 0.2267 for chunks 0 to 13, more for the rest. The chunk's buffer alone does not settle it: in the changed kernel's first plain part chunks 12 and 13 take 0.2267 each for tile 0, then 0.2283 and 0.2320 for tile 1. The runs here do not tell why.
